# A decoder layer's output projection: joined products of 512 columns, and four moved pieces

## The chip, the cores and the metric

The kernel runs on one core of a Trainium2 chip. A core has a matrix engine (TensorE, "PE" in the profile, with its weight loads as "PEld"), VectorE (DVE), ScalarE (ACT), GpSimd (POOL) and SyncE (SP, which issues transfers). Matrix products write to PSUM, eight banks of 512 float32 per partition; everything else lies in SBUF, and weights come from HBM by DMA. The metric is the device time of one execution in microseconds, as the median of several runs.

## The reference, cut to what matters

One decoder layer on 256 rows of 1024, with two attention mixers side by side. What the change touches is the merge and the output projection:

```python
h = rmsnorm(x, norm1_g)
proj = h @ w_in          # q, k/v of three branches, branch gates, MoBA q/k/v, merge gates
y_nsa = nsa_attention(...)      # compressed + selected + sliding-window branches
y_moba = moba_attention(...)
gm = sigmoid(g_m)
mixed = g_nsa * (y_nsa @ w_up_nsa) + g_moba * (y_moba @ w_up_moba)
x = x + mixed @ w_out
h2 = rmsnorm(x, norm2_g)
u = relu(h2 @ w_ff1)
x = x + (u * u) @ w_ff2
return rmsnorm(x, norm_f_g)
```

Everything is float32, and the result has to agree with float32.

## The kernel before, in words

**Split products.** TensorE is used with operands rounded to a shorter float32 form (F32R). To keep the accuracy, each operand is split in a high part (the rounded value) and a low part (the rest, rounded): for weights `hi[c]` and `lo[c]`, for activations `hTh`/`hTl`, `yTh`/`yTl`, `mxh`/`mxl`, `h2h`/`h2l`, and `ah`/`al` for the squares. A product is then three: high x high, high x low and low x high (`mm3`, L264). High parts are made by ScalarE copies (L113), low parts by VectorE subtractions (L115).

**Weight chunks and slots.** The weights come in 60 chunks (`CHUNKS`) of mostly 128 x 2048. A chunk's products form a slot: a list of matrix products in order, which `run_slot` (L235) writes out while it drops other work in between. That other work is given by `at(pos, f, ...)`: f's instructions are written once the fraction pos of the slot's products stands. So the order on every engine is that of this one program; each engine runs its own instructions strictly in that order, and waits where an operand is not ready. Equal positions keep the order in which they were given. `split_events` (L303) places, in slot c, the two halves of the split of chunk c + 2 (high by ScalarE, low by VectorE) and the load of chunk c + 6, which reuses the buffer that the split of c + 2 has read.

**The slots in order.** Key/value chunks 0 to 3; q, MoBA q, k and v (4 to 11, `xstat`: activations stationary, weights moving, 384 to 512 columns); merge gates (12 to 19); up-projections (20 to 23); the output projection `w_out` (24 to 27); then the feed-forward part, ff1 and ff2 chunks in turn from 28 on. From 12 to 30 it is `wstat` (L293): a 128 x 128 weight block is stationary, and 256 columns of activations move. ff2 products are formed by a scheme with seven products in place of eight (`seven_mms`), whose operand sums VectorE makes (`sums`).

**Warm-up.** Before the first data arrive, TensorE does 14 transposes of the identity (L160). Then the first 48 products of chunks 0 and 1 follow the splits of their quarters (loop at L197).

**Attention inside the slots.** The six attention units (`PAIRS`) run inside slots 9 to 21 (`unit_events`, L653): scores (`d_scores`) into the banks Sa and Sb, row maximum (`d_max`), exponentials (`d_exp`), normalisation (`d_norm`), transposes of the probabilities back into Sa and Sb with copies to `PT` by ScalarE (L611) and VectorE (L613) (`d_trans`), the compressed branch's product (`d_cmp`), probabilities x values (`d_pv`), and the split of the result (`d_yevac`). The scores of the next unit need Sa and Sb free again. In slot 13 the split of chunk 15 stands at 0.0 and 0.06, and `d_trans` at 0.06, given after it.

**Merge gates.** Each gate slot's result is scaled by VectorE out of PSUM (`gm_evac`, L803), at 0.02 of the next slot, and its tanh follows on ScalarE at once (L809). The up-projections use it as sigmoid.

**Output projection.** In each of four slots two blocks of 128 output columns are formed over eight inner blocks, three products each (`two_blocks`, L785, and for the last slot L936 to L940). `wout_evac` (L893) then adds the result to the residual on VectorE (L896), makes `h2h` on ScalarE (L900) and `h2l` on VectorE (L903). In the first projection slot VectorE also finishes the mixed rows (`upm_evac`, `mix_l`, L835 to L843).

**Banks.** Accumulators rotate over the banks named in `turn["acc"]`: acc0, tp and acc1 in the gates, up-projections and output projection. In slots 25 and 26 both blocks share one bank; in 24 and 27 each has its own.

Of the kernel before, what the change touches and what calls it, by code (L numbers as in the profile page):

```python
# [14 lines left out]
NEG = -3.0e38  # L15
NWARM = 14
EPS = 1e-6
# [27 lines left out]
def hybrid_layer(ctx: ExitStack, tc: tile.TileContext, gxd, w, w1c, small, const, gf, out):  # L45
# [112 lines left out]
    warm = bank("yb", "yb")  # L158
    for _ in range(NWARM):
        pe.transpose(warm[:, 0:128], ident, ident)  # L160
    dve.tensor_reduce(gsum, ident.rearrange("p (g i) -> p i g", g=4), op=ALU.add, axis=AX)
    pool.memset(ones, 1.0)
# [21 lines left out]

    def act_tiles(name):
        return [cp.tile([128, 2048 + e], F32R, name=name + n, tag="act" + n.upper())
                for n, e in (("h", 128), ("l", 16))]

    def act_views(tiles, o):
        return (a[:, o:o + 2048].rearrange("p (k q) -> p k q", k=8) for a in tiles)  # L190

    h_tiles = act_tiles("hT")
    hTh, hTl = act_views(h_tiles, 16)

    for kt in range(8):  # L197
        act.activation(hTh[:, kt, :], xT[:, kt, :], AF.Copy, scale=g1[:, kt:kt + 1])
        if kt == 0:
            hi[0] = wp.tile([128, 2048], F32R, name="whi")  # L200
            lo[0] = wp.tile([128, 2048], F32R, name="wlo")
            dve.tensor_copy(hi[0][:, 0:384], raw[0][:, 0:384])
# [56 lines left out]
    def mm(o, l, r, start, stop):  # L259
        if len(r.shape) > len(o.shape):  # L260
            o = o.rearrange("p (b a) -> p b a", a=2)
        pe.matmul(o, l, r, start=start, stop=stop, skip_group_check=True)  # L262
# [30 lines left out]
    def wstat(o, c, off, nk, ncol, ah, al, ks=None, first=0, last=None):  # L293
# [7 lines left out]
        return r  # L301

    def split_events(c, hs, ls):  # L303
        for i in range(2):
# [7 lines left out]
    def std_events(c):  # L312
# [4 lines left out]
        elif 9 <= c < 20 and c % 2:  # L317
            split_events(c, (0.0, 0.06), (0.09, 0.46))
        elif 9 <= c < 20:
            split_events(c, (0.0, 0.45), (0.3, 0.8 if c > 10 else 0.92))  # L320
        else:
            split_events(c, (0.0, 0.45), (0.3, 0.46))
# [272 lines left out]

    def d_trans(d):

        S, P = U[d]["S"], U[d]["P"]
        kind, p, _ = PAIRS[d][0]
        PT = ap_.tile([128, 4, 384], F32, name="PT")  # L600
        U[d]["PT"] = PT
        v = PT.rearrange("p (x j) k -> p j x k", x=2)
        for t, cs in ((1, (128, 256)), (0, (0,))):
            T = s_views(d, t)
            for j in range(2):
                for x in range(2):
                    for c in cs:
                        o = c % 256 if t == 0 else c - 128
                        pe.transpose(T[:, j, x, o:o + 128], P[:, 2 * x + j, c:c + 128], ident)  # L609
            if t:  # L610
                act.activation(v[:, :, :, 128:384], T, AF.Copy)  # L611
            else:
                dve.tensor_copy(v[:, :, :, 0:128], T)  # L613
        if d == 0:
            U["y"] = bank("yb", "yb").rearrange("p (a q) -> p a q", a=2)

    def d_cmp(d):
# [35 lines left out]
    def unit_events(s):  # L653
# [11 lines left out]
        if d > 0:  # L665
            at(0.1 + late, d_cmp, d - 1)
        if d < 6:
# [15 lines left out]
    for k in range(4):  # L683
        for c, n, accs in ((0, 384, first), (1, 408, second)):
            m = xstat(c, n, accs, range(4), [k])
            mms += m if k else [m[i] for i in (0, 3, 1, 4, 2, 5)]
    at(0.6, load, 6)
# [115 lines left out]
    def gm_evac(g, outs, whole):  # L803
        if g == 4:
            sgs.append(ap_.tile([128, 8, 256], F32, name="sgb", tag="w1"))
        v = sgs[g // 4][:, 2 * (g % 4):2 * (g % 4) + 2]
        dve.tensor_tensor(v, whole.rearrange("p (m q) -> p m q", m=2),
                          U["rows"][:, None, :].to_broadcast([128, 2, 256]), op=ALU.mult)
        act.activation(v, v, AF.Tanh, scale=0.5)  # L809

    prev = [(evac_tm, ("vm", 1, accs[1], 512))]
    turn["acc"] = ["acc0", "tp", "acc1"]
    for g in range(8):
# [3 lines left out]
        for f, a in prev:  # L817
            at(0.02, f, *a)
        mms, outs, whole = two_blocks(c, hTh, hTl)
        run_slot(mms)  # L820
        prev = [(gm_evac, (g, outs, whole))]

    mxh, mxl = act_views(act_tiles("mx"), 0)

# [20 lines left out]
    for sec, c0, kind, evac in (("upn", C_UPN, "n", upn_evac), ("upm", C_UPM, "m", upm_evac)):  # L845
        for i in range(2):
            c = c0 + i
            if c == C_UPN:
                split_events(c, (0.3, 0.3), (0.4, 0.4))
            elif c == C_UPM:  # L850
# [42 lines left out]
    def wout_evac(i, outs, ms=(0, 1)):  # L893
        for m in ms:
            k = 2 * i + m
            dve.tensor_tensor(tok(x1T[:, k, :]), tok(xT[:, k, :]), tok(outs[m], True),  # L896
                              op=ALU.add)
        for m in ms:
# [22 lines left out]
    for i in range(4):  # L921
# [9 lines left out]
        if i == 1:  # L931
            at(0.01, open_ff)
            for j in range(4):
                at(0.9, gamma_rows, j)
        if i == 3:
            outs = [acc_tile()[:, 0:256] for _ in range(2)]  # L936
            at(0.52, wout_evac, i, outs, (0,))
            run_slot([m for j in range(2)
                      for m in wstat(outs[j], c, j * 128, 8, 256, mxh, mxl)])
            prev = [(wout_evac, (i, outs, (1,)))]  # L940
        else:
            mms, outs, _ = two_blocks(c, mxh, mxl, 6 if i == 0 else 8)
            run_slot(mms)
            prev = [(wout_evac, (i, outs))]

# [60 lines left out]
    def wt_tile(shape, dtype, name, i):  # L1006

        if i % 3 == 2:
            return cp.tile(shape, dtype, name=name + "c", tag="actH")
        return FB["p"].tile(shape, dtype, name=name, tag="wt", bufs=2)  # L1010
# [316 lines left out]
```

## Time and profile before

| | |
|---|---|
| median of 3 runs | 355.59 us (355.57 to 355.95) |
| the profiled execution's own time | 355.47 us |
| its span in the profile | 353.7 us |
| granted TensorE clock, mean | 0.994 |
| PE busy | 345.8 us (98% of the span), 2667 products |
| VectorE busy | 309.7 us (88%) |
| ScalarE busy | 240.0 us (68%) |
| DMA | 73.69 MB, 208 GB/s on average |

The span runs from the first to the last instruction that the profiler saw; the rest of the time lies around it. A busy matrix engine in the profile is not one at its peak, since products are pipelined; the spacing from one product's start to the next tells more. A row of the order of time reads: start, length, engine, line, operation, output <- input, shape, count, and in brackets the idle time before it and what ended it.

### The profile page before, as it was taken

The numbers are of one execution on the slowest core, as the hardware profiler recorded it, in microseconds if no ns is written. First come the engines' busy times: TensorE is split into PE (matmuls) and PEld (weight loads), VectorE is DVE, ScalarE is ACT, GpSimd is POOL, SyncE is SP. The second block draws the span as 40 slices with busy tenths as digits, with TensorE's granted clock in tenths as the row PEclk, the third lists the DMA queues.
The fourth block names the chain that finished last, engine by engine and source line by source line (L and its number), as shares of the span: only waits on it lengthen the run. The fifth ranks groups of instructions, "written<-read, shape, count | busy, mean of one in ns | idle before, by whom it ended". The sixth has DMA issues, their size and how long they took to land.

```text
span 353.7 us, 6540 instructions
## 1 busy us (share of the span) xinstructions
PE 345.8 (98%) x2667; PEld 324.7 (92%) x2667; DVE 309.7 (88%) x420; ACT 240.0 (68%) x358; POOL 26.0 (7%) x46
## 2 busy tenths in 40 slices
PE   8999999999999999999999999999999999999993
PEld 7998788888999999999999999999999999999982
DVE  5989789877886878966978999999999999999794
ACT  6994665866656757636566988977777788776713
POOL 1010000000000000000311111101110111000001
PEclk9999999999999999999999999999999999999997
DMA  8999525345333334433697978788888888870003
GB/s 268 416 420 349 193 78 225 119 155 205 117 122 120 120 120 170 188 120 119 202 308 220 371 205 285 243 282 279 259 262 279 290 277 274 237 278 39 0 2 120
DMA packets 14880, 73.69 MB, mean 208 GB/s; under 512 B 1793, under 2 KB 3713, under 8 KB 7553
## 3 DMA queue, kind: packets, MB, share of 16 engines
q1 hardware_dynamic: 11088, 64.88, 49.8%
q0 software_dynamic: 3328, 7.87, 10.2%
q10 hardware_dynamic: 432, 0.52, 0.4%
q8 instruction: 21, 0.34, 0.4%
q14 instruction: 11, 0.08, 0.1%
HBM read 72.21 MB, written 1.05 MB: 207 GB/s over the span
## 4 chain that ended last, share of the span: by engine, by line
PE 91%; DVE 4%; ACT 2%; issue 2%; POOL 0%; POOLq 0%; DVEq 0%
PE acc L262 60%; PE o L262 10%; PE yb L262 5%; PE tp L262 3%; PE qacc L262 3%; PE kvbacc L262 3%; PE Sa L262 2%; PE Sa L609 1%; PE tp L364 1%; PE yb L160 1%; DVE wlo L115 1%; PE Sb L609 1%; DVE x L1062 1%; PE Sb L262 1%; PE o L917 0%
## 5 line engine op out<-in xcount | busy, mean ns | idle before, releaser
L115 DVE TENSOR_TENSOR wlo<-raw,whi 128x1024 fp32r<-128x1024 f32 (+4 forms) x85 | 105.3, 1260 | 2.8 <-ACT whi L113 2.6
L113 ACT ACTIVATE whi<-raw 128x1024 fp32r<-128x1024 f32 (+4 forms) x84 | 90.5, 1096 | 20.8 <-PE acc L262 11.8
L262 PE MATMUL acc<-h2h,whi 128*128 128x256 f32 x256 | 70.5, 275 | 0.0
L262 PE MATMUL acc<-h2l,whi 128*128 128x256 f32 x256 | 70.4, 275 | 0.0
L262 PE MATMUL acc<-h2h,wlo 128*128 128x256 f32 x256 | 70.4, 275 | 0.0
L262 PEld LDWEIGHTS acc<-h2l,whi 128*128 128x128 f32 x256 | 49.2, 192 | 0.0
L262 PEld LDWEIGHTS acc<-h2h,wlo 128*128 128x128 f32 x256 | 49.2, 192 | 0.0
L262 PEld LDWEIGHTS acc<-h2h,whi 128*128 128x128 f32 x256 | 49.1, 192 | 0.0
L262 PE MATMUL acc<-hTh,wlo 128*128 128x256 f32 x128 | 35.7, 279 | 0.0
L262 PE MATMUL acc<-hTl,whi 128*128 128x256 f32 x128 | 35.3, 276 | 0.0
L262 PE MATMUL acc<-hTh,whi 128*128 128x256 f32 x128 | 35.3, 276 | 0.0
L1033 ACT ACTIVATE whi<-wt 128x2048 fp32r<-128x2048 f32 x10 | 19.2, 1918 | 18.7 <-PE acc L262 18.2
L262 PEld LDWEIGHTS acc<-hTh,wlo 128*128 128x128 f32 x128 | 24.5, 192 | 0.5 <-issue 0.5
L262 PEld LDWEIGHTS acc<-hTl,whi 128*128 128x128 f32 x128 | 24.6, 192 | 0.2 <-issue 0.2
L1026 DVE TENSOR_TENSOR sl<-raw,sh 128x1536 fp32r<-128x1536 f32 x14 | 24.6, 1758 | 0.0
L262 PEld LDWEIGHTS acc<-hTh,whi 128*128 128x128 f32 x128 | 24.6, 192 | 0.0
L262 PE MATMUL acc<-whi,hTh 128*128 128x512 f32 (+2 forms) x65 | 24.3, 377 | 0.0
L262 PE MATMUL acc<-wlo,hTh 128*128 128x512 f32 (+2 forms) x65 | 23.8, 368 | 0.0
L262 PE MATMUL acc<-whi,hTl 128*128 128x512 f32 (+2 forms) x65 | 23.6, 365 | 0.0
L1035 DVE TENSOR_TENSOR wlo<-wt,whi 128x2048 fp32r<-128x2048 f32 x10 | 22.9, 2293 | 0.7 <-ACT whi L1033 0.3
L1024 ACT ACTIVATE sh<-raw 128x1536 fp32r<-128x1536 f32 x14 | 20.7, 1480 | 0.0
L262 PE MATMUL acc<-mxl,whi 128*128 128x256 f32 x64 | 17.7, 276 | 0.0
(323 smaller groups left out, 893.2 us busy)
## 6 DMA issues: line engine op xcount, KB each, us to landing
raw<-in_ff_dram SPq DMA_DIRECT2D x32, 1024.0 KB, 6.3
raw<-in_gm_dram SPq DMA_DIRECT2D x8, 1024.0 KB, 4.8
wt<-in_ff_dram POOLq DMA_DIRECT2D x20, 256.0 KB, 7.3
raw<-in_wout_dram SPq DMA_DIRECT2D x4, 1024.0 KB, 4.8
raw<-in_q_dram SPq DMA_DIRECT2D x2, 1024.0 KB, 8.5
raw<-in_qm_dram SPq DMA_DIRECT2D x2, 1024.0 KB, 8.8
raw<-in_km_dram SPq DMA_DIRECT2D x2, 1024.0 KB, 7.5
raw<-in_vm_dram SPq DMA_DIRECT2D x2, 1024.0 KB, 6.3
```

The source lines that it names most:

```text
L113: act.activation(hi[c][:, a:b], raw[c][:, a:b], AF.Copy)
L115: dve.tensor_tensor(lo[c][:, a:b], raw[c][:, a:b], hi[c][:, a:b].bitcast(F32), op=ALU.subtract)
L160: pe.transpose(warm[:, 0:128], ident, ident)
L262: pe.matmul(o, l, r, start=start, stop=stop, skip_group_check=True)
L364: pe.transpose(tp[:, j * 256 + t * 128:j * 256 + t * 128 + 128], src[:, t, (2 * i + j) * 128:(2 * i + j + 1) * 128], ident)
L609: pe.transpose(T[:, j, x, o:o + 128], P[:, 2 * x + j, c:c + 128], ident)
L1024: act.activation(singles[c][0], v, AF.Copy)
L1026: dve.tensor_tensor(singles[c][1], v, singles[c][0].bitcast(F32), op=ALU.subtract)
L1033: act.activation(hi[c], v, AF.Copy)
L1035: dve.tensor_tensor(lo[c], v, hi[c].bitcast(F32), op=ALU.subtract)
L1062: dve.scalar_tensor_tensor(x1[:, t, s], y, fst[:, 4 + t:5 + t], x1[:, t, s], op0=ALU.mult, op1=ALU.add)
```

## The change

In the output projection one product takes the high weights against both parts of the mixed rows (512 moving columns, written to a whole bank: the high part's sum in the first 256 columns, the low part's in the last 256), and a second takes the low weights against the high part, added to the first 256 columns. Both parts of the activations now lie in one tile, `act`. Each output block has its own bank, and a fourth bank (yb) joins the rotation. `wout_evac` adds the two halves of the bank one after the other.

Beside it: the warm-up is 8 transposes and 9 products on a rounded copy of the identity; within a group of six in slots 0 and 1 the products with the low weights come last; `d_trans` is written as `d_turn` and `d_turned`, with both copies behind all transposes; in slot 13 the second half of the split stands at 0.07; in slot 11 `d_cmp` stands at 0.125 in place of 0.14; and the gates' tanh stands at 0.47 of the next slot in place of directly behind its multiply.

```diff
-NWARM = 14
+NWARM = 8, 9
...
-    for _ in range(NWARM):
+    for _ in range(NWARM[0]):
         pe.transpose(warm[:, 0:128], ident, ident)
+    for c in range(3):
+        hi[c] = wp.tile([128, 2048], F32R, name="whi")
+        lo[c] = wp.tile([128, 2048], F32R, name="wlo")
+    r = hi[2][:, 0:128]
+    dve.tensor_copy(r, ident)
+    for _ in range(NWARM[1]):
+        pe.matmul(warm[:, 0:128], r, r, start=True, stop=True, skip_group_check=True)
...
-    def act_tiles(name):
-        return [cp.tile([128, 2048 + e], F32R, name=name + n, tag="act" + n.upper())
-                for n, e in (("h", 128), ("l", 16))]
...
+    def act_tile(name, o=0):
+        v = cp.tile([128, 4240], F32R, name=name, tag="act")[:, o:o + 4096]
+        return v.rearrange("p (x k q) -> p x k q", x=2, k=8)
...
+    def wstat2(o, c, off, a, ks):
+        r = []
+        for k in ks:
+            w = slice(k * 256 + off, k * 256 + off + 128)
+            both = a[:, :, k, :].rearrange("p x (a b) -> p x b a", a=2)
+            m = [lambda w=w, both=both, k=k: mm(o, hi[c][:, w], both, k == 0, k == 7),
+                 lambda w=w, k=k: mm(o[:, 0:256], lo[c][:, w], paired(a[:, 0, k, :]), False, False)]
+            r += m if k < 7 else m[::-1]
+        return r
...
-            split_events(c, (0.0, 0.06), (0.09, 0.46))
+            split_events(c, (0.0, 0.07 if c == 13 else 0.06), (0.09, 0.46))
...
-    def d_trans(d):
+    def d_turn(d):
...
-            if t:
-                act.activation(v[:, :, :, 128:384], T, AF.Copy)
-            else:
-                dve.tensor_copy(v[:, :, :, 0:128], T)
...
+    def d_turned(d):
+        v = U[d]["PT"].rearrange("p (x j) k -> p j x k", x=2)
+        act.activation(v[:, :, :, 128:384], s_views(d, 1), AF.Copy)
+        dve.tensor_copy(v[:, :, :, 0:128], s_views(d, 0))
...
-            at(0.1 + late, d_cmp, d - 1)
+            at(0.125 if s == 11 else 0.1 + late, d_cmp, d - 1)
...
-            mms += m if k else [m[i] for i in (0, 3, 1, 4, 2, 5)]
+            mms += [m[i] for i in ((0, 3, 2, 5, 1, 4) if k or c else (0, 3, 1, 4, 2, 5))]
...
+
+    def gm_tanh(g):
+        v = sgs[g // 4][:, 2 * (g % 4):2 * (g % 4) + 2]
         act.activation(v, v, AF.Tanh, scale=0.5)
...
+        if g:
+            at(0.47, gm_tanh, g - 1)
...
             if c == C_UPN:
+                at(0.47, gm_tanh, 7)
...
-            dve.tensor_tensor(tok(x1T[:, k, :]), tok(xT[:, k, :]), tok(outs[m], True),
-                              op=ALU.add)
+            for x in range(2):
+                dve.tensor_tensor(tok(x1T[:, k, :]), tok((x1T if x else xT)[:, k, :]),
+                                  tok(outs[m][:, 256 * x:256 * x + 256], True), op=ALU.add)
...
+        if i == 0:
+            turn["acc"].append("yb")
+        outs = [acc_tile() for _ in range(2)]
+        ks = (range(6), range(6, 8)) if i == 0 else (range(8),)
         if i == 3:
-            outs = [acc_tile()[:, 0:256] for _ in range(2)]
             at(0.52, wout_evac, i, outs, (0,))
-            run_slot([m for j in range(2)
-                      for m in wstat(outs[j], c, j * 128, 8, 256, mxh, mxl)])
-            prev = [(wout_evac, (i, outs, (1,)))]
-        else:
-            mms, outs, _ = two_blocks(c, mxh, mxl, 6 if i == 0 else 8)
-            run_slot(mms)
-            prev = [(wout_evac, (i, outs))]
+        run_slot([m for s in ks for j in range(2) for m in wstat2(outs[j], c, j * 128, mx, s)])
+        prev = [(wout_evac, (i, outs, (1,) if i == 3 else (0, 1)))]
```

In the groups of six, indices 0 to 2 are the first 128 rows' products (high x high, high rows x low weights, low rows x high weights) and 3 to 5 the same of the second 128 rows.

More of the change, by code (lines that the diff above doesn't have):

```diff
@@ L178, in hybrid_layer @@
     cmpm = kc_[:, K_CMP:K_CMP + 30].rearrange("p (t i) -> p t i", t=2)
-    def act_tiles(name):
-        return [cp.tile([128, 2048 + e], F32R, name=name + n, tag="act" + n.upper())
-                for n, e in (("h", 128), ("l", 16))]
[L189 to L195, printed above, removed]
+    def act_tile(name, o=0):
+        v = cp.tile([128, 4240], F32R, name=name, tag="act")[:, o:o + 4096]
+        return v.rearrange("p (x k q) -> p x k q", x=2, k=8)
+    hT = act_tile("hT", 16)
+    hTh, hTl = hT[:, 0], hT[:, 1]
     for kt in range(8):
@@ L199, in hybrid_layer @@
         if kt == 0:
-            hi[0] = wp.tile([128, 2048], F32R, name="whi")
-            lo[0] = wp.tile([128, 2048], F32R, name="wlo")
             dve.tensor_copy(hi[0][:, 0:384], raw[0][:, 0:384])
@@ L259, in mm @@
     def mm(o, l, r, start, stop):
-        if len(r.shape) > len(o.shape):
+        if len(r.shape) == 4:
+            o = o.rearrange("p (x b a) -> p x b a", x=2, a=2)
+        elif len(r.shape) > len(o.shape):
             o = o.rearrange("p (b a) -> p b a", a=2)
@@ L594, in d_norm @@
                               op=ALU.mult)
-    def d_trans(d):
+    def d_turn(d):
         S, P = U[d]["S"], U[d]["P"]
[L599 to L602, printed above, removed]
+        U[d]["PT"] = ap_.tile([128, 4, 384], F32, name="PT")
         for t, cs in ((1, (128, 256)), (0, (0,))):
@@ L609, in d_trans @@
                         pe.transpose(T[:, j, x, o:o + 128], P[:, 2 * x + j, c:c + 128], ident)
-            if t:
-                act.activation(v[:, :, :, 128:384], T, AF.Copy)
-            else:
-                dve.tensor_copy(v[:, :, :, 0:128], T)
         if d == 0:
             U["y"] = bank("yb", "yb").rearrange("p (a q) -> p a q", a=2)
+    def d_turned(d):
+        v = U[d]["PT"].rearrange("p (x j) k -> p j x k", x=2)
+        act.activation(v[:, :, :, 128:384], s_views(d, 1), AF.Copy)
+        dve.tensor_copy(v[:, :, :, 0:128], s_views(d, 0))
+    def d_trans(d):
+        d_turn(d)
+        d_turned(d)
     def d_cmp(d):
@@ L821, in hybrid_layer @@
         prev = [(gm_evac, (g, outs, whole))]
-    mxh, mxl = act_views(act_tiles("mx"), 0)
+    mx = act_tile("mx")
+    mxh, mxl = mx[:, 0], mx[:, 1]
     def up_views(k):
@@ L1008, in wt_tile @@
         if i % 3 == 2:
-            return cp.tile(shape, dtype, name=name + "c", tag="actH")
+            v = cp.tile([128, 4240], dtype, name=name + "c", tag="act")[:, 0:2048]
+            return v.rearrange("p (b n) -> p b n", b=4) if len(shape) == 3 else v
         return FB["p"].tile(shape, dtype, name=name, tag="wt", bufs=2)
```

## The prediction

> **What bounds the kernel now.** I read the page first, then the busy time by stage, then PE's own order of time for places where its spacing grows, and last the queues of VectorE (DVE) and ScalarE (ACT) at those places.
>
> ```profile
> span 353.7 us, 6540 instructions
> ...
> PE 345.8 (98%) x2667; PEld 324.7 (92%) x2667; DVE 309.7 (88%) x420; ACT 240.0 (68%) x358; POOL 26.0 (7%) x46
> ...
> PE 91%; DVE 4%; ACT 2%; issue 2%; POOL 0%; POOLq 0%; DVEq 0%
> ...
> 169.67:175.04 5.37, 5.37 (x50) 5.37 (x49) 5.06 (x9) 2.95 (x4) 2.43 (x5) 1.00 0.72 243
> ...
> 203.75:213.66 9.91, 9.91 (x73) 9.40 (x72) 9.91 (x11) 7.43 (x8) 1.44 (x2) 1.00 0.81 241
> ```
>
> The third row is the chain that ended last: 91% of it is TensorE (PE). The last two are stages (length, then busy PE, weight load, DVE, ACT, POOL). In the second slot of the output projection (169.67 to 175.04) PE is never idle, but DVE has 5.06 us of work in 5.37; in the feed-forward part (203.75 on) DVE is as full as PE. So PE sets the time, with DVE close behind exactly where this change gives DVE more to do. The sum therefore has three places: the start, one stall near 86 us, and the projection with what follows it.
>
> **The start: warm-up and the order of the first products.**
>
> ```profile
> 1.36 3.25 PE L160 MATMUL yb<-ident 128*128 128x128 f32 x14 [1.36 <-POOL ones L162]
> ...
> 3.83 0.36 DVE L202 CAST whi<-raw 128x384 fp32r<-128x384 f32 x1 [2.11 <-DMA raw<-in_kva_dram]
> ...
> 4.33 0.87 PE L262 MATMUL acc<-whi,hTh 128*128 128x384 f32 x2
> ...
> 5.04 0.49 PE L262 MATMUL acc<-wlo,hTh 128*128 128x384 f32 x2
> ...
> 5.44 0.58 DVE L115 TENSOR_TENSOR wlo<-raw,whi 128x408 fp32r<-128x408 f32 x1 [0.26 <-ACT whi L113]
> ...
> 6.08 0.30 PEld L262 LDWEIGHTS kvbacc<-wlo,hTh 128*128 128x128 f32 x2 [0.20 <-DVE wlo L115]
> ...
> 6.87 0.33 PE L262 MATMUL acc<-whi,hTh 128*128 128x384 f32 x1
> ...
> 7.04 0.43 PE L262 MATMUL acc<-wlo,hTh 128*128 128x384 f32 x1
> 7.15 0.19 PEld L262 LDWEIGHTS acc<-whi,hTl 128*128 128x128 f32 x1
> 7.31 0.33 PE L262 MATMUL acc<-whi,hTl 128*128 128x384 f32 x1
> ```
>
> Fourteen transposes take 3.25 us (about 0.21 each, the first 0.27). The first operand that PE needs, whi, is ready at 3.83 + 0.36 = 4.19. The new warm-up is eight transposes (until about 3.1) and nine 128-column products on a copy that DVE makes while it is idle. A 128-column product is not in the trace on all 128 rows; two full-rate products of 384 columns took (5.04 - 4.33) = 0.71 together here, half-speed ones included, so 128 columns cost between 0.11 (0.71 / 6) and the transposes' 0.21. The warm-up then ends between 4.1 and 5.0. I take the lower end, since the product streams its columns once and its weight load can run under the product ahead of it, as it does later in this kernel. Then data at about 4.25 sets the first product, and PE gains about 0.1 of useful time (the transposes' tail ran to 4.6 by the first row). At the upper end PE loses about 0.25.
>
> The new order puts the products with the low weights last in each group of six. Two waits go. DVE delivers wlo at 5.44 + 0.58 = 6.02, and the weight load for it starts at 6.08 after 0.20 of idle; of this I count 0.15, since a product was still running. And 7.04 to 7.31 is 0.27 for a product, again one on fresh wlo, where the one ahead of it took 0.17 (6.87 to 7.04): 0.10, the weight load that could not run ahead. In the new order both wlo come two products before their use. What is late next is whi of the following quarter, which has the same lead as before within 0.1. Sum of the start: **-0.33** (between -0.40 and +0.07).
>
> By the Trainium skill ("TensorE: Matmul & The Clock Gate", Part 4: PE-mode transpose) a transpose does not count as busy for the clock in the same way as a product. By that rule the transposes before 4.33 would not have opened the clock, but the two products at 5.04 lie 0.16 apart (0.49 for two of 0.33), 0.7 us after the first of all; the trace does not bear it out, and the sum stays.
>
> **The stall at 86 us.** In slot 13 (the second chunk of the merge gates) ACT has, in order, half a weight copy, the gates' tanh, the other half, and the copy of the turned probabilities.
>
> ```profile
> 83.25 1.06 ACT L113 ACTIVATE whi<-raw 128x1024 fp32r<-128x1024 f32 x1 [1.51 <-issue]
> ...
> 83.45 1.04 PE L609 MATMUL Sa<-ident,P 128*128 128x128 f32 x8
> ...
> 84.69 0.63 ACT L809 ACTIVATE sga<-sga 128x512 f32<-128x512 f32 x1 [0.37 <-DVE sga L807]
> 85.22 1.04 ACT L113 ACTIVATE whi<-raw 128x1024 fp32r<-128x1024 f32 x1
> 86.17 1.01 ACT L611 ACTIVATE PT<-Sa 128x1024 f32<-128x1024 f32 x1
> ...
> 86.45 0.28 PE L262 MATMUL yb<-pcT,bdvl 128*128 128x256 f32 x1
> 87.23 0.50 PE L262 MATMUL Sa<-kswh,qrh 64*128 64x512 f32 x2 [0.49 <-ACT PT L611]
> ```
> ```profile
> 70.00 0.28 PE L262 MATMUL yb<-pcT,bdvl 128*128 128x256 f32 x1
> 70.21 0.51 PE L262 MATMUL Sa<-kswh,qrh 64*128 64x512 f32 x2
> ```
>
> The scores reuse the bank that the ACT copy (L611) reads, so PE goes from 86.45 to 87.23, 0.78, where the same step without a wait took 70.21 - 70.00 = 0.21. With the split moved from 0.06 to 0.07 the copy stands ahead of the second half, and the tanh is far behind: the transposes end at 83.45 + 1.04 = 84.49, the copy at 85.5, one us before PE wants the bank. The second half of the weight copy then ends at 86.5 instead of 86.26; its chunk is used two slots (over 10 us) later. **-0.57**, and I see no second wait behind it, so between -0.45 and -0.60.
>
> The tanh at 0.47 is 0.63 of ACT work in every gate slot, no longer waiting for DVE ahead of ACT's other work. Its result is read in the up-projections, a slot or more later, and the bank is freed by the DVE multiply, which stays. The three d_cmp products in slot 11 only change places with four transposes; splitting d_trans leaves each engine's order as it is; one tile for both parts has the size of the two. All at 0; if the cover of the tanh failed, it would cost its 0.63 once.
>
> **The projection.** Each of the 64 pairs "high weights times high rows, high weights times low rows" becomes one product.
>
> ```profile
> 203.59 0.38 PE L262 MATMUL o<-sh,ah 128*128 128x512 f32 x1
> 203.81 0.38 PE L262 MATMUL o<-sl,ah 128*128 128x512 f32 x1
> 204.02 0.38 PE L262 MATMUL o<-sh,al 128*128 128x512 f32 x1
> ```
> ```profile
> 164.34 0.28 PE L262 MATMUL acc<-mxl,whi 128*128 128x256 f32 x1
> 164.45 0.28 PE L262 MATMUL acc<-mxh,wlo 128*128 128x256 f32 x1
> 164.57 0.28 PE L262 MATMUL acc<-mxh,whi 128*128 128x256 f32 x1
> ```
>
> 512 columns are spaced 0.216, 256 columns 0.112. So a pair costs 0.216 for 0.223: 64 x 0.0075 = 0.5 us. The weight load saved was already hidden. In the first slot about 0.15 goes again, since the joined product needs the low rows of block 6 a product earlier, and those come late from DVE. PE alone: **-0.34**.
>
> The Trainium skill ("TensorE: Matmul & The Clock Gate", Back-to-back issue gap) gives 131 ns for a sustained 512-column product. By that the pairs would save 5.9 us; the rows above say 216 ns, and I go by them.
>
> The price is on DVE: each 128x256 block of the residual is now added in two steps, the second on the result of the first, eight additions more.
>
> ```profile
> 165.53 0.68 DVE L835 SCALAR_TENSOR_TENSOR sgb<-sgb,acc 128x512 f32<-128x512 f32 x1
> 166.24 0.69 DVE L836 TENSOR_TENSOR sga<-sga,sgb 128x512 f32<-128x512 f32 x1
> ...
> 170.80 0.74 DVE L896 TENSOR_TENSOR gx<-gx,acc 128x256 f32<-128x256 f32 x2
> 171.85 0.89 DVE L903 SCALAR_TENSOR_TENSOR h2l<-gx,h2h 128x256 fp32r<-128x256 f32 x2 [0.31 <-ACT h2h L900]
> ...
> 185.96 0.42 DVE L896 TENSOR_TENSOR gx<-gx,acc 128x256 f32<-128x256 f32 x1 [1.19 <-PE acc L262]
> ...
> 193.71 0.69 DVE L1003 TENSOR_TENSOR wt<-raw,wt 128x512 f32<-128x512 f32 x1
> ...
> 194.43 1.92 ACT L1033 ACTIVATE whi<-wt 128x2048 fp32r<-128x2048 f32 x1 [0.51 <-DVE wt L1003]
> ...
> 199.89 0.43 DVE L999 TENSOR_TENSOR aq<-aq 128x256 f32<-128x256 f32 x1 [0.61 <-ACT aq L961]
> ...
> 201.84 1.09 DVE L977 TENSOR_TENSOR al<-aq,ah 128x896 fp32r<-128x896 f32 x1
> ```
>
> Two independent additions take 0.74, so the second costs 0.32. A dependent one starts only after its predecessor: L836 at 166.24 follows L835's end (166.21) by 0.03. So an in-place addition costs 0.42 + 0.03 = 0.45, and eight cost 3.6. What absorbs them: the 1.19 in which DVE waits for PE at 185.96; about 0.4 of the waits for h2h within the three evacuations of two blocks (0.31 at 171.85; the second block still waits for its own copy); and about 0.4 in smaller gaps. The 0.61 at 199.89 hardly helps: ACT's L1033 waits for L1003, and behind it stand the four copies of the turned rows and the squares that L999 waits for, so ACT is late with DVE. About 3.6 - 2.0 = 1.64 of lateness is left when DVE reaches `al`, the low part of the first squares. It ends at 201.84 + 1.09 = 202.93 today, and the product at 204.02 needs it. New end 204.57, and 0.05 for the release: that product starts 0.60 later than today, whatever PE gained before. The 0.34 is swallowed, and the projection's net is **+0.60** (from -0.34, nothing late, to +1.5). ACT and SyncE follow: the weight loads issued behind late splits land up to 1.9 later, on chunks that are split two slots before their use, so I put them at 0. After 204 I count no further wait: PE itself has moved back by then, and what DVE makes next is for later slots.
>
> Sum: -0.33 - 0.57 + 0.60 = -0.30. The profiled execution took 355.47 (span 353.7), 0.12 under the median of the runs, 355.59; on the median this gives **355.3**.
>
> **The rivals.**
>
> (1) The added additions overlap like the independent ones, 0.32 each: 2.6 in place of 3.6, lateness 0.64, `al` at 203.6, when PE (0.34 earlier) wants it at 203.7. Then the stall is gone: -0.33 - 0.57 - 0.34 = -1.24, **354.35**. For it: the stall is less than 1 us on a lateness built from many rows. Against it: L835 to L836. The Trainium skill ("VectorE: DVE Perf Modes", The DRAIN you can't avoid) says that a semaphore between two DVE operations costs nothing extra, which would make both kinds cost the same; the trace has 0.32 against 0.45.
>
> (2) Slower: the sixteen additions take not 0.42 but 0.50, as the L903 operation of the same shape nearly does (0.89 for two). That is 1.36 more lateness: h2h and h2l of the last block reach PE late in the first feed-forward slot, and `al` later still; total about +1.0, **356.6**. It is slower than before, beyond what can be measured, from about 0.48 on. Against it: L896 itself shows 0.42 twice.
>
> (3) Slower, at the start: the clock opens later because the warm-up has a gap before 4.25. If it opened later by as much as the old warm-up lasts (3.25), half of that is lost: 355.3 + 1.6 = **356.9**. Against it: PE stays busy from 1.36 in both.
>
> **How the numbers follow.** The forecast gets 0.50, with its own range 354.8 to 355.9; rival (1) 0.31; rival (2) 0.10; rival (3) 0.04; 0.05 is for the start bringing nothing, about 355.6. What can be told from no change is 0.2%, 0.71 us: 354.88 to 356.30. Faster: rival (1) and 0.07 from the forecast's lower edge, 0.38. Slower: rivals (2) and (3) less a little, 0.13. The same: 0.49. The range reaches to rival (1) and its edge and close to rival (2): 354.2 to 356.5.
>
> **What would show it.** Start: no idle of the weight load at wlo around 6, and spacing 0.16 from 6.6 on. Slot 13: L611's copy directly behind the first half copy, and 0.21 in place of 0.78. Projection: slots of about 5.24 where 5.37 stands; L896 in fours of about 1.56; a wait of PE for `al` of nearly 1 us before that product (near 203.7 in the new trace, since the first two places shift it by 0.9). If PE has no wait there, rival (1) holds. If PE already waits for h2l in the first feed-forward slot, rival (2). The prediction is wrong in its basis if the joined products are not spaced 0.216.

## The result, and the profile after

The changed kernel takes **360.56 us** (357.58 to 361.4) against 355.58 for the one before on the same chip: ratio **1.0118, interval 1.0094 to 1.0142**. I had forecast 355.3, with a range up to 356.5. The profiled execution took 360.04, with a span of 358.2 against 353.7. Two executions far from all others (602.78 us of the kernel before, beside e9 to e12, and 1273.13 us of e4) are left out of the ratios.

The page of the changed kernel: span, busy times, the chain that ended last by engine, and one group (count, then busy time and mean ns of one, then the idle time before them and what ended it).

```profile
span 358.2 us, 6432 instructions
...
PE 348.2 (97%) x2606; PEld 325.3 (91%) x2606; DVE 312.9 (87%) x429; ACT 239.0 (67%) x358; POOL 26.1 (7%) x46
...
PE 91%; DVE 4%; ACT 2%; issue 1%; POOL 0%; POOLq 0%; DVEq 0%; ACTq 0%
...
L266 PE MATMUL acc<-mx,whi 128*128 128x512 f32 x64 | 22.3, 403 | 2.7 <-ACT mx L861 2.7
```

PE (TensorE) has 61 products fewer and is busy 2.4 us *longer*; so its products ran slower somewhere, and the last row names a wait that the kernel before did not have. I followed the same products through both traces and noted by how much each starts later or earlier:

| first product of | before, us | after, us | shift | shift added by this part |
|---|---|---|---|---|
| chunk 0 (first real product) | 4.33 | 4.95 | +0.61 | |
| q (all of the start is done) | 21.53 | 22.67 | +1.14 | **+1.14** |
| third scores (behind slot 13) | 87.23 | 87.80 | +0.57 | **-0.57** |
| output projection | 164.23 | 165.31 | +1.08 | **+0.51** |
| feed-forward part | 185.76 | 190.35 | +4.59 | **+3.51** |
| `sh,al` | 204.02 | 208.61 | +4.58 | -0.01 |
| end of the span | 353.7 | 358.2 | +4.58 | 0.00 |

So the loss arises at the start and in the first slot of the output projection. The start, as PE's order of time (start, length, engine, line, operation, operands, shape, count):

```profile
2.99 2.16 PE L167 MATMUL yb<-whi 128*128 128x128 f32 x9
4.95 0.95 PE L266 MATMUL acc<-whi,hT 128*128 128x384 f32 x2
5.69 0.85 PE L266 MATMUL acc<-wlo,hT 128*128 128x384 f32 x2
6.33 0.85 PE L266 MATMUL acc<-whi,hT 128*128 128x384 f32 x2
6.97 1.00 PE L266 MATMUL kvbacc<-whi,hT 128*128 128x408 f32 x4
```

Nine warm-up products fill the time from 2.99 to 4.95, 0.22 each. Then pairs of 384-column products follow each other by 0.64 (5.69 to 6.33), 0.32 each; only within the last row, from about 7.3, does the spacing become 0.17. In the kernel before, one product was spaced 0.16 from 5.04 on. The trace's own record of the granted clock begins, at full speed, at 7.26 here and at 4.96 in the kernel before; so that is when the clock opened. (A table by stage shows 1.00 before this first record too, where nothing was recorded; the spacing shows the half clock there.)

This accounts for the start. The first product is 0.61 later. PE then works at half clock for 2.31 us (4.95 to 7.26) in place of 0.63 (4.33 to 4.96); each microsecond of it costs half (0.32 against 0.16 a product), so the longer stretch costs 0.84. The waits on `wlo` that the new order was to remove, about 0.25, are gone. Together +1.20, against +1.14 measured.

Slot 13, the turned probabilities' copy, the compressed branch and the next scores:

```profile
85.72 1.02 ACT L628 ACTIVATE PT<-Sa 128x1024 f32<-128x1024 f32 x1 [0.27 <-PE Sa L622]
...
87.59 0.28 PE L266 MATMUL yb<-pcT,bdvl 128*128 128x256 f32 x1
...
87.80 0.50 PE L266 MATMUL Sa<-kswh,qrh 64*128 64x512 f32 x2
```

ScalarE's copy now ends at 86.74, and the scores follow the product at 87.59 by 0.21 instead of 0.78.

The first slot of the output projection, PE's order of time, then ScalarE's (ACT), then VectorE's (DVE):

```profile
164.70 0.28 PE L266 MATMUL acc<-yThm,wlo 128*128 128x256 f32 x1
165.31 0.48 PE L266 MATMUL acc<-mx,whi 128*128 128x512 f32 x1 [0.33 <-ACT mx L861]
165.63 0.27 PE L266 MATMUL acc<-mx,wlo 128*128 128x256 f32 x1
168.22 0.80 PE L266 MATMUL acc<-mx,whi 128*128 128x512 f32 x1 [2.32 <-ACT mx L861]
...
169.02 0.64 PE L266 MATMUL acc<-mx,whi 128*128 128x512 f32 x1
169.45 0.42 PE L266 MATMUL acc<-mx,wlo 128*128 128x256 f32 x1
...
171.24 0.27 PE L266 MATMUL acc<-mx,wlo 128*128 128x256 f32 x1
171.35 0.38 PE L266 MATMUL acc<-mx,whi 128*128 128x512 f32 x1
171.57 0.27 PE L266 MATMUL acc<-mx,wlo 128*128 128x256 f32 x1
```
```profile
164.54 0.72 ACT L861 ACTIVATE mx<-sga 128x512 fp32r<-128x512 f32 x1 [2.19 <-DVE sga L860]
...
167.51 0.66 ACT L861 ACTIVATE mx<-sga 128x512 fp32r<-128x512 f32 x1 [1.30 <-DVE sga L860]
```
```profile
165.29 0.81 DVE L866 SCALAR_TENSOR_TENSOR mx<-sga,mx 128x256 fp32r<-128x256 f32 x2 [0.78 <-ACT mx L861]
...
168.20 0.76 DVE L866 SCALAR_TENSOR_TENSOR mx<-sga,mx 128x256 fp32r<-128x256 f32 x2 [0.79 <-ACT mx L861]
```

L861 writes two blocks of the mixed rows' high part at a time. The first joined product reads block 0 of both parts and starts when the copy of blocks 4 and 5 has ended (164.54 + 0.72 = 165.26). The second reads block 1 and starts at 168.22, when the copy of blocks **6 and 7** has ended (168.17). Neither reads those blocks. In the program the copy of 4 and 5 stands ahead of the first joined product, and the copy of 6 and 7 between the first and the second, which is why the two wait for different copies. The low rows of the same blocks (L866) also stand ahead of these products, but both products start while VectorE is still writing them (165.31 within 165.29 to 166.10, 168.22 within 168.20 to 168.96). So it is not the whole tile that a joined product waits for: high blocks 4 to 7 lie between the two parts that it reads, low blocks 4 to 7 behind them.

And after this wait a joined product takes 0.43 to the next start (169.02 to 169.45), twice the 0.22 of 171.35 to 171.57. The busy time by stage shows the cause (length, busy PE, weight load, DVE, ACT, POOL, granted clock, DMA):

```profile
167.90:171.30 3.40, 3.08 (x10) 2.70 (x11) 3.03 (x4) 1.21 (x2) 1.59 (x3) 0.53 0.04 16
171.30:176.00 4.70, 4.70 (x31) 4.33 (x30) 1.59 (x4) 1.12 (x2) 1.12 (x3) 1.00 0.97 318
```

The granted clock was 0.53 over the first stretch and 1.00 over the second; the trace records the half clock from 167.69 to 171.10, so it began while PE was still waiting. In sum: the second wait costs 2.59 - 0.11 = 2.48 (165.63 to 168.22, where 0.11 is the normal spacing). The half clock costs 1.49: from 168.22 to 171.24 stand five joined products and four single ones in 3.02, where five of 0.2185 and four of 0.109 would have taken 1.53. Together 3.97; the other 0.46 to the 3.51 of the table is what the joined products gave back (64 times 0.3345 - 0.3275, a block's three products against its two, is 0.45).

Not every execution paid for the half clock. A stretch of 3.41 us lowers the mean granted clock of an execution by 0.005. The one at 357.58 has a mean of 0.996, the other three have 0.991 to 0.993; in e2 below, two at 357.80 and 357.87 have 0.997, the other four 0.993 to 0.994. That these three had the wait without the half clock behind it is likely, but no trace of them was kept.

At `al` nothing waits now:

```profile
208.39 0.38 PE L266 MATMUL o<-sl,ah 128*128 128x512 f32 x1
208.61 0.38 PE L266 MATMUL o<-sh,al 128*128 128x512 f32 x1
```

### The profile page after: what moved, and what is told of

Same layout as the page of the kernel before. It is cut to its first block, busy times and chain, and to the rows that moved or that the text cites. A ratio compares the mean times of both kernels' runs of the same rounds, so it can differ in the third digit from the quotient of the medians.

```text
span 358.2 us, 6432 instructions
## 1 busy us (share of the span) xinstructions
PE 348.2 (97%) x2606; PEld 325.3 (91%) x2606; DVE 312.9 (87%) x429; ACT 239.0 (67%) x358; POOL 26.1 (7%) x46
## 4 chain that ended last, share of the span: by engine, by line
PE 91%; DVE 4%; ACT 2%; issue 1%; POOL 0%; POOLq 0%; DVEq 0%; ACTq 0%
PE acc L266 60%; PE o L266 9%; PE yb L266 5%; PE tp L266 3%; PE qacc L266 3%; PE kvbacc L266 3%; PE Sa L266 2%; PE Sa L622 1%; PE tp L380 1%; PE Sb L622 1%; DVE x L1087 1%; PE Sb L266 1%; ACT mx L861 1%; ACT whi L113 1%; PE yb L160 1%
## 5 line engine op out<-in xcount | busy, mean ns | idle before, releaser
L266 PE MATMUL acc<-hT,whi 128*128 128x256 f32 x256 | 43.6, 276 | 0.0
L266 PEld LDWEIGHTS acc<-hT,whi 128*128 128x128 f32 x256 | 38.9, 192 | 0.2 <-issue 0.2
L266 PE MATMUL acc<-whi,hT 128*128 128x512 f32 (+2 forms) x130 | 38.5, 375 | 0.0
L266 PE MATMUL acc<-hT,wlo 128*128 128x256 f32 x128 | 35.7, 279 | 0.0
L266 PEld LDWEIGHTS acc<-whi,hT 128*128 128x128 f32 x130 | 24.4, 194 | 3.0 <-issue 0.6
L266 PEld LDWEIGHTS acc<-hT,wlo 128*128 128x128 f32 x128 | 24.5, 192 | 0.5 <-issue 0.5
L266 PE MATMUL acc<-mx,whi 128*128 128x512 f32 x64 | 22.3, 403 | 2.7 <-ACT mx L861 2.7
L266 PE MATMUL acc<-wlo,hT 128*128 128x512 f32 (+2 forms) x65 | 23.5, 373 | 0.0
L266 PE MATMUL acc<-mx,wlo 128*128 128x256 f32 x64 | 16.7, 282 | 0.0
L266 PEld LDWEIGHTS acc<-mx,whi 128*128 128x128 f32 x64 | 12.3, 200 | 4.6 <-ACT mx L861 3.1
```

## The experiments

Three readings had to be told apart: a wait of the joined products that the data do not need; the warm-up; and whether the step on VectorE that I had predicted is absent or only covered by PE's being late. Line numbers shift by up to two between these kernels. Unless told otherwise each was run in five rounds beside the kernel before.

**e1: only the layout of the mixed rows changed.** The changed kernel with the parts of one block next to each other, block by block, in place of all high blocks ahead of all low ones. The joined product's operand is then one short stretch.

```diff
-    mx = act_tile("mx")
-    mxh, mxl = mx[:, 0], mx[:, 1]
+    mx = cp.tile([128, 4240], F32R, name="mx", tag="act")[:, 0:4096]
+    mx = mx.rearrange("p (k x q) -> p k x q", x=2, k=8)
+    mxh, mxl = mx[:, :, 0], mx[:, :, 1]
```

> Edit: the changed kernel with one thing altered: the mixed rows lie block by block (high and low part of a block side by side) in place of all high parts ahead of all low parts, so that the joined product reads one unbroken stretch. Span theory: the wait at the second joined product (2.32 us on ScalarE's last high part) stands there because the read from a high block to its low block is ordered behind every write in between. Then the 0.33 and 2.32 us of waits and the half clock behind them go, the first joined product follows the up-projection within 0.15 us, and the time falls by about 4 us minus what VectorE's lateness gives back: 355.8 to 357 us at a start like the profiled one (1.14 us late). Rival, late data: the product really lacks its rows; the wait stays over 2 us and the time stays about 360.

Measured: 357.45, ratio 1.0042 (1.0031 to 1.0053). From the projection's first product to the feed-forward part's first the shift changes by -0.17 in place of +3.51, and that first product is itself no longer late. The start is worse in this profile, +2.49, where the expectation had gone by +1.14; so the time lies a little above its range. Products near 7 to 10 us:

```profile
6.97 1.57 PE L266 MATMUL kvbacc<-whi,hT 128*128 128x408 f32 x4
...
9.01 1.30 PE L266 MATMUL acc<-whi,hT 128*128 128x384 f32 x4
10.15 0.49 PE L266 MATMUL acc<-wlo,hT 128*128 128x384 f32 x2
```

Half spacing (0.34 for 408 columns, 0.32 for 384) lasts until about 10 us (the record has 9.99), with the same instructions that reached full speed at 7.3 in the changed kernel's profile.

**e2: only the old warm-up put back.**

```diff
-NWARM = 8, 9
+NWARM = 14, 0
...
-    r = hi[2][:, 0:128]
-    dve.tensor_copy(r, ident)
```

> Edit: the changed kernel with the old warm-up (14 transposes, no products). Warm-up theory: nine 128-column products cost 0.213 us each at half clock, so the first real product starts 0.6 us late, and the clock opens near 7.3 in place of 5.0 us; with the old warm-up the start is 0.2 to 0.4 us ahead of before, since the new order of the first groups remains, and the stretch at 165 us stays: about 358.5 to 359. Rival, chance: the late opening of the clock is the phase of the moment and not the warm-up; then times here still scatter by more than 1 us between runs for the start alone, and the median stays near 360.

Measured: 359.04, ratio 1.0080 (1.0061 to 1.0099). The start is back (+0.06), but not ahead as expected: the clock opens at 4.38, which gains 0.3 on the kernel before, and PE loses it again in waits for `wlo` and the row squares. The wait in the projection is the same, and so is the slow stretch behind it:

```profile
164.53 0.27 PE L264 MATMUL acc<-mx,wlo 128*128 128x256 f32 x1
167.12 0.48 PE L264 MATMUL acc<-mx,whi 128*128 128x512 f32 x1 [2.32 <-ACT mx L859]
```
```profile
167.00:168.30 1.30, 1.18 (x7) 1.10 (x8) 1.20 (x3) 1.01 (x2) 0.00 (x0) 0.97 0.00 0
168.30:171.70 3.40, 3.40 (x12) 2.95 (x12) 1.89 (x2) 0.00 (x0) 2.71 (x5) 0.51 0.41 111
```

Here PE ran 1.1 us at full speed before the clock fell (167.12 to 168.22; the record has half clock from 168.22 to 171.63): the half clock lasts 3.4 us again, but begins after the wait. By the Trainium skill ("TensorE: Matmul & The Clock Gate", HAM oscillation — how this bites in real kernels) the rule is to have no idle gaps of PE above about 3.4 us; here one of 2.5 us was enough. What the Trainium skill says there of a free-running window of 3.4 us (What's actually happening, in Part 1) agrees with the length of the stretch and with its different distance from the wait.

**e3: both.** The block-by-block layout and the old warm-up.

> Edit: both of the last two together. Expected: 355.59 - 0.25 (order of the first groups) - 0.57 (slot 13) and then either + 0.60 (VectorE's in-place additions make the low part of the first squares late, the prediction's step) = 355.4, or - 0.34 (they do not) = 354.4. In the first case PE waits nearly 1 us ahead of the third product of ff2's first slot, in the second there is no wait there. If the two waits at 165 us had another cause than those two theories, the time stays above 357.

Measured: 355.87, above both times expected; ratio 1.0000 (0.9991 to 1.0008). PE's order of time at the two places:

```profile
164.19 0.28 PE L264 MATMUL acc<-yThm,wlo 128*128 128x256 f32 x1
164.30 0.38 PE L264 MATMUL acc<-mx,whi 128*128 128x512 f32 x1
164.52 0.27 PE L264 MATMUL acc<-mx,wlo 128*128 128x256 f32 x1
164.63 0.38 PE L264 MATMUL acc<-mx,whi 128*128 128x512 f32 x1
...
168.12 0.27 PE L264 MATMUL acc<-mx,wlo 128*128 128x256 f32 x1
168.53 0.48 PE L264 MATMUL acc<-mx,whi 128*128 128x512 f32 x1
...
203.70 0.38 PE L264 MATMUL o<-sl,ah 128*128 128x512 f32 x1
204.61 0.48 PE L264 MATMUL o<-sh,al 128*128 128x512 f32 x1 [0.53 <-DVE al L1000]
```

The false wait is gone. What is left at 168.12 is a gap of 0.41, the low rows of block 6 that VectorE delivers late, which the joined product does read. And now the wait on `al` that I had predicted is there: 0.91 from 203.70 to 204.61. In the changed kernel, PE's 2.5 us of waiting and its slow stretch had given VectorE the time.

The start is +0.65 in this profile in spite of the old warm-up. About 0.3 of it is the clock, which opened at 5.51 with the same 14 transposes that had opened it at 4.96 (1.25 us at half clock in place of 0.63). Besides, PE now waits in a place that was full before:

```profile
17.95 1.15 DVE L220 TENSOR_TENSOR xsq<-xsq 128x512 f32<-128x512 f32 x2
...
18.28 0.51 PE L264 MATMUL kvbacc<-whi,hT 128*128 128x408 f32 x2
...
19.24 0.58 PE L264 MATMUL tp<-ones,xsq 128*128 128x2 f32 x4 [0.46 <-DVE xsq L220]
```

The sums of the row squares end at 19.10, and the product that needs them follows at 19.24, where 18.62 would have been its turn. So PE loses 0.62 here, more than the 0.25 of waits on `wlo` that the new order of the first products removed.

**e4: only the new warm-up, in the kernel before.**

> Edit: the kernel before with the new warm-up alone (8 transposes, 9 products on the rounded identity). Warm-up theory: 1.0 to 1.4 us slower, 356.6 to 357.0, the first real product near 4.95 us. Rival, chance: same as before within 0.4 in the median, with a wider scatter.

Measured: 357.74, ratio 1.0041 (1.0024 to 1.0058), the same as e1. First product +0.61, q +2.33, full speed from 9.7 us, the rest unchanged. The warm-up's cost does not depend on the rest of the change.

**e5: only slot 13, in the kernel before.** The tanh of the gates moved, a split at 0.07, the compressed branch's product at 0.125.

> The kernel before with the moved tanh of the gates and the two moved positions of the slot (a split at 0.07, a mask at 0.125), nothing else of the change. Slot theory: PE's wait of 0.77 us ahead of the third score products is gone, these start 0.57 us earlier, and nothing after them gives it back: about 355.0, ratio 0.9984. Rival (the gain is given back later): the third score products 0.57 earlier, the first product of the output projection and the end as before, ratio 1.000.

Measured: 355.28, ratio **0.9984** (0.9976 to 0.9993). The scores start 0.63 earlier, and the end is 0.72 earlier (0.05 of it from the start): nothing gives it back.

```profile
86.39 0.28 PE L262 MATMUL yb<-pcT,bdvl 128*128 128x256 f32 x1
86.60 0.50 PE L262 MATMUL Sa<-kswh,qrh 64*128 64x512 f32 x2
```

**e6: e3 with `ah` and `al` first.** ScalarE and VectorE make the two parts of the first squares ahead of the row squares and of the second set of operand sums.

```diff
-                at(0.03, act_parts, 0, "h")
-                at(0.07, act_parts, 0, "l")
+                at(0.01, act_parts, 0, "h")
+                at(0.04, act_parts, 0, "l")
```

> The changed kernel with parts laid out block by block and the old warm-up (e3), and in it ScalarE's and VectorE's two instructions that make the feed-forward's first ah and al issued ahead of the row squares and of the second set of sums. Lateness theory: e3's wait of 0.91 us on al is there because VectorE, filled up by the eight added additions, comes to al late; with al first, the wait is gone and the end is 0.9 us earlier than e3's: 354.9, ratio 0.9975. Rival (VectorE is the bound from there on): PE waits as long a little later for the second chunk's sums, ratio 1.000.

Measured: 355.71, ratio 0.9994 (0.9985 to 1.0002), between the two expectations. The product on `al` follows without a wait, but a little later there is a new one:

```profile
208.05 0.28 PE L264 MATMUL acc<-h2l,whi 128*128 128x256 f32 x1
208.54 0.38 PE L264 MATMUL acc<-h2h,wlo 128*128 128x256 f32 x1 [0.21 <-DVE wlo L115]
```

PE waits for the low weights, which stand behind the moved `al` on VectorE: 0.49 - 0.11 = 0.38. A queue that is full hands its lateness to whatever comes next in it.

**e7: e3 with the additions apart.** First both blocks' high rows, then both blocks' low rows.

```diff
-        for m in ms:
-            k = 2 * i + m
-            for x in range(2):
+        for x in range(2):
+            for m in ms:
+                k = 2 * i + m
```

> e3 with the four additions of a slot in another order, first both blocks' high rows, then both blocks' low rows, so that no addition follows the one it depends on. Dependence theory (0.45 us from start to start behind the addition it depends on, 0.34 otherwise): the four start within 1.0 us instead of 1.23 us in three slots, up to 0.66 us in all, less what is lost again waiting for ScalarE's copy, so the wait on al falls from 0.91 to 0.25 to 0.6 us: 355.2 to 355.5, ratio 0.9982 to 0.9991. Rival (the number of additions decides, not their order): the wait stays at 0.9 and the time at e3's, ratio 1.000.

Measured: 355.48, ratio 0.9991 (0.9982 to 0.9999). VectorE's order of time at the first additions, in e3 and then in e7:

```profile
170.98 1.65 DVE L921 TENSOR_TENSOR gx<-gx,acc 128x256 f32<-128x256 f32 x4
...
173.21 0.48 DVE L928 SCALAR_TENSOR_TENSOR h2l<-gx,h2h 128x256 fp32r<-128x256 f32 x1 [0.18 <-ACT h2h L925]
```
```profile
170.88 1.40 DVE L921 TENSOR_TENSOR gx<-gx,acc 128x256 f32<-128x256 f32 x4
172.59 0.89 DVE L928 SCALAR_TENSOR_TENSOR h2l<-gx,h2h 128x256 fp32r<-128x256 f32 x2 [0.31 <-ACT h2h L925]
```

Four take 1.40 in place of 1.65; between starts it is 0.34 where an addition is independent and 0.45 where it follows the one it depends on. Part of this goes into waiting for ScalarE's copy (0.31 in place of 0.18). The gap ahead of the product on `al` falls from 0.91 to 0.43 (0.22 of it is the normal spacing), as the dependence theory had it.

**e8: eight transposes and six rounded products** (e1 with the shorter warm-up, which ends when the old one ends).

```diff
-NWARM = 8, 9
+NWARM = 8, 6
```

> The block-by-block layout (e1) with eight warm-up transposes and six rounded products instead of eight and nine, which last as long as the fourteen transposes of before, so that the first real product starts at 4.3 us, as in e3. Kind theory (rounded products of 128 columns do less to open the clock than transposes): the clock opens at 7 us or later as in e1, and the start loses 0.6 us or more against e3: ratio 1.002 to 1.004. Time theory (only the later first product cost): the clock opens between 4.5 and 5.7 us as in e3, ratio 1.000.

Measured: 356.27, ratio 1.0013 (1.0001 to 1.0025), single runs from 355.46 to 357.85. The profile is that of the fastest of them; in it the first real product starts at 4.31 and full speed comes at 5.5, as in e3. It fits the time theory, but the spread of 2.4 us does not: e3's runs lie within 0.9. That would fit six rounded products that delay the clock in some executions and not in others, but one trace can't show it.

**e9: seventeen transposes** (e3 with a warm-up as long as the new one, and no rounded product).

```diff
-NWARM = 14, 0
+NWARM = 17, 0
```

> e3 with seventeen transposes in the warm-up in place of fourteen: as long as eight transposes and nine rounded products, with no rounded product in it. Time theory (the new warm-up costs only because the first real product starts at 4.95 us in place of 4.3): like e1, first product at 4.9 to 5.0, clock open at 7 to 10 us, ratio 1.004. Kind theory (the rounded products hold the clock back): first product at 4.9 to 5.0, but the clock opens between 4.5 and 6 us as in e3, loss 0.3 to 0.6 us, ratio 1.001 to 1.002, and the single runs lie within 1 us of each other.

Measured: 356.53, ratio 1.0014 (1.0005 to 1.0023), single runs from 355.8 to 356.81. The first product starts at 4.91, and full speed comes at 7.1 in the profile, later than the kind theory had said; the ratio and the spread are the kind theory's. One profile can't decide this, since with 14 transposes the clock opened anywhere from 4.4 to 7.1; the ratios do, each against the kernel before on the same chip, as e9's interval ends below e1's. So, as an estimate from the ratios, about a third of the warm-up's 0.0042 is its length, as 0.0014 shows, and two thirds the rounded products. Why these hold the clock back, no run shows.

**e10: e3 with e6 and e7 together.**

> e3 with the additions apart (e7) and al first (e6). Lateness theory: e7 has left 0.21 us of the wait on al, and e6 without the shorter additions paid 0.33 us for a wait on wlo at 208 us, because its second sums were late; together both waits are gone and the end is 0.2 us earlier than e7's: 355.2, ratio 0.9985. Rival (VectorE stays the bound from 200 us on): one of the two waits is still there with 0.2 us or more, ratio 0.999 or above.

Measured: 355.31, ratio **0.9977** (0.9968 to 0.9986). In its profile the clock opened at 7.09, which alone costs about 1.0 us at the start, so the profiled execution ends no earlier than that of the kernel before; the gain shows in the ratio. Both waits are gone:

```profile
203.81 0.38 PE L264 MATMUL o<-sl,ah 128*128 128x512 f32 x1
204.03 0.38 PE L264 MATMUL o<-sh,al 128*128 128x512 f32 x1
```

**e11: e10 with the product of the row squares later in its slot.**

```diff
-    at(0.4, row_norm)
+    at(0.55, row_norm)
```

and what hangs on it moved along, 0.15 each.

> e10 with the products of the row squares and what hangs on them issued later in their slot (0.55 in place of 0.4, about 0.65 us). Start theory: with the order of the first products changed, PE comes to the row squares' product too early (gaps of 0.45 to 0.79 us there in e2, e3 and e7) and hands back what it gained; issued later, that gap is gone, qacc starts 0.3 to 0.6 us earlier than in e10 and the end with it: 354.7 to 354.9, ratio 0.997 to 0.9975. Rival (ScalarE and VectorE carry the lateness on to the next slot): PE waits as long in the next slot, ratio as e10.

Measured: 355.07, ratio **0.9974** (0.9964 to 0.9984), the fastest here, but not told apart from e10. The rival is right in kind: PE no longer waits for the squares, as it does in e2, e3 and e7, but for the low weights that VectorE makes after them. (In e10's profile there is no wait at the squares, since PE came to them late.) The start, +0.28 against e10's +0.79, doesn't price this edit: here the clock opened at 5.00.

```profile
18.54 0.51 PE L264 MATMUL kvbacc<-whi,hT 128*128 128x408 f32 x2
19.36 0.44 PE L264 MATMUL kvbacc<-wlo,hT 128*128 128x408 f32 x1 [0.31 <-DVE wlo L115]
```

**e12: the other parts without joined products.** The kernel before with slot 13, the new order of the first products and the later row squares.

> The kernel before with the other parts alone: slot 13, the order of the first products, and the row squares later as in e11; the output projection as before, with no joined product. If the joined products gain PE 0.34 us net once nothing waits for them, this ends 0.3 us behind e11: 355.0 to 355.2, ratio 0.998 to 0.9985. Rival (the added additions take the whole gain): same time as e11 or earlier.

Measured: 355.19, ratio **0.9975** (0.9964 to 0.9986), against 0.9974 for e11. From the projection's first product to the feed-forward part's first e11 gains 0.16 and e12 0.09 on the kernel before. So the joined products gain 0.07 us in the profiles once no false wait stands before them; the medians differ by 0.12, where each interval is 0.35 wide to either side. A gain from them isn't shown.

## Why the prediction was wrong, point by point

By places, as shifts against the kernel before in the profiled executions (us). Each row is what that place adds; the forecast for `al` is its net +0.60 less the -0.34 of the products alone.

| place | forecast | changed kernel | e2 | e3 | e10 |
|---|---|---|---|---|---|
| start | -0.33 | +1.14 | +0.06 | +0.65 | +0.79 |
| slot 13 | -0.57 | -0.57 | -0.58 | -0.58 | -0.58 |
| joined products, first block | 0 | +0.51 | +0.50 | +0.01 | +0.01 |
| joined products, the rest | -0.34 | +3.51 | +3.78 | -0.17 | -0.21 |
| `al` | +0.94 | -0.01 | 0 | +0.69 | 0 |
| behind it | 0 | 0 | 0 | +0.10 | +0.02 |
| end | -0.30 | +4.58 | +3.76 | +0.69 | +0.02 |

The first row is one execution each and holds a part that is not the edit's: with 14 transposes the clock opened at 4.38, 5.51 and 7.09 in e2, e3 and e10 and at 4.96 in the kernel before, which is worth -0.3, +0.3 and +1.0 us.

- **"One tile for both parts has the size of the two. All at 0" is the step that failed, with 4.0 of the 4.6 us.** I looked at the tile's size and not at what its layout does to the order of the program. The joined product's operand reaches from block k of the high half to block k of the low half, across all blocks that lie between. The second joined product started with the end of the last copy into that stretch, though it reads none of it; with the blocks next to each other (e1, and e3 against e2), the only edit, the wait is gone. That the ordering goes by the stretch's two ends is the reading that fits both starts, the low rows outside the stretch that were not waited for, and the disappearance of the wait; I did not test other layouts.
- **The half clock** behind that wait was in no part of the prediction. It made a wait of 2.5 us cost 4.0 in the profiled execution.
- **The start, -0.33.** Two terms were wrong. The nine products were taken at the lower bound, 0.11; they took 0.22, the transposes' price at the upper end, which I had worked out and set aside. So the first product is 0.61 late, not early. And rival (3), a clock that opens later, which I gave 0.04, came true: 7.3 us in the changed kernel, 9.7 and 10.0 in e4 and e1, against 4.4 to 7.1 with the old warm-up. It did not come by the gap that the rival named: I had argued against it that PE stays busy from 1.36 in both. It does, and the clock still opened later; e9 against e1 shows that the kind of work counts, not only that there is some. The 0.25 for two waits on `wlo` was right, and the changed kernel has it, because its clock opens so late that PE waits for nothing else. Where the clock opens early it is no gain: PE runs into the row squares (0.28, 0.62 and 0.60 in e2, e3 and e7), and moved past those, into the next low weights (e11). There VectorE sets the time at 19 us.
- **Slot 13, -0.57:** right in place and size, in every kernel that has it, and kept to the end (e5).
- **The joined products, -0.34.** The gross gain of 0.48 is right: it was 0.46 in the changed kernel. For the late low rows of block 6 I had counted 0.15; e3 shows 0.41 - 0.11 = 0.30 (168.12 to 168.53), so -0.17 is left.
- **`al`, a wait of nearly 1 us.** Not in the changed kernel, so by the test I had set, "if PE has no wait there, rival (1) holds", I would have concluded that the additions overlap. That test was bad, since another wait can hide this one. e3 shows 0.91 - 0.22 = 0.69 of it, with dependent additions at 0.45, as forecast; the lateness was sized right within 0.3. Rival (1) is refuted by e3's spacing and by e7: apart, the additions cost 0.34, and the gap falls to 0.43.
- **Small slips in the sums,** none of which changes the account: the three terms of the start add to 0.35, not 0.33; 3.6 - 2.0 is 1.6, not 1.64; sixteen additions at 0.08 more are 1.28, not 1.36. And the two first products of 384 columns, 0.71 together, ran mostly at half clock (until 4.96), not at the full rate.

With the false wait and the warm-up taken out (e3), the kernel is equal to the one before; the forecast of -0.30 lies at the edge of what e3's interval allows (-0.32 to +0.28).

## What to carry to other kernels

When two operands are put in one tile so that one instruction can read both, ask what lies between them, who writes that and when; put them next to each other. Waits add up by queue, not by place: where two engines are both nearly full, a removed wait shows up at the next thing that the other engine delivers, and a predicted wait may be hidden by a larger one, so price each change alone. And cost an operation that no row shows by the nearest row of the same shape, not by a proportion of larger ones.

## What the runs showed of the hardware

- A gap of 2.5 us in PE's work was followed by 3.4 us at half clock (0.51 and 0.53 granted in the tables by stage), in both kernels that had it (changed kernel, e2). The half clock began 0.5 us before the gap's end in one and after 1.1 us of full speed in the other, and by the mean clocks it did not come in every execution.
- In all fourteen traces the granted clock stayed at full speed for a whole multiple of 3.413 us from its opening or return to its next fall (47, 48, 54, 101 or 102 times); the half clock in between lasted 3.413 us.
- Rounded products of 128 columns were spaced as the transposes were, 0.21 to 0.22, at the start. With eight transposes and nine of them the clock opened at 7.3, 9.7 and 10.0 us (changed kernel, e4, e1); with 17 transposes at 7.1 (e9); with 14 between 4.4 and 7.1 in nine profiles, in eight of them by 6.2. The Trainium skill ("TensorE: Matmul & The Clock Gate", Part 4: PE-mode transpose) says that the full clock does not engage for transposes, since they don't count as busy in the same way; the runs do not agree. In e2 the clock opened at 4.38, when PE had done nothing but transposes until 4.35.
- An addition on VectorE of 128x256 that reads the result of the one ahead of it starts 0.45 after it, an independent one 0.34 (e3, e7).
